# A gMLP and forgetting-attention trunk on one core: the samples' spatial weights turned on VectorE, and the forget gate's running sums as column tiles

## The chip, the core and the metric

The kernel runs on one of the eight cores of a Trainium2 chip. A core has TensorE (PE in the profile: matrix products, and transposes as products with an identity matrix; PEld is its loading of weights), VectorE (DVE), ScalarE (ACT), GpSimd (POOL) and SyncE (SP), which here only issues transfers. Each engine works through its own instructions in order and waits at semaphores for the others. Transfers can also be issued from ScalarE's and GpSimd's queues. SBUF is the on-chip memory with 128 partitions; PSUM is the memory of eight banks into which TensorE writes.

The metric is the device time of one execution in microseconds (us). The times are a median of three runs; the profile is of one execution.

## The reference

One inference step of a two-layer encoder. There are two groups of tokens: a prompt of 512 tokens, and 8 samples of 16 tokens each, 640 tokens in all, which the kernel treats as five tiles of 128 (the fifth holds the samples). Model width 1024, branch width E = 2048. What matters here:

```python
# layer 0, gMLP
proj = h @ w_in                          # (tokens, 3E)
uv = gelu(proj[..., :2*E]); z = proj[..., 2*E:]
u = uv[..., :E]
v = layer_norm(uv[..., E:], ln_g, ln_b)
n = min(T, 128)                          # prompt: blocks of 128; samples: one block of 16
wm = where(chunk_causal_mask(n), w_s[:, :n, :n], 0)
s = einsum('gij,bnjgc->bnigc', wm, vb) + b_s[:, :n].T[...]
y = u * s * silu(z);  out = y @ w_out
# layer 1, forgetting attention
q, k, v, z, logf = ...                   # logf = log_sigmoid(h @ w_f + b_f), one per token and head
cT = cumsum(logf, axis=1).transpose(...) # running sums, 16 heads
s = q @ k * scale + cT[query] - cT[key]; softmax over the causal keys; @ v; * silu(z); @ w_out
```

In layer 0 there are 16 groups g of 128 channels, each with its own 128 x 128 matrix w_s[g]. The samples use the top left 16 x 16 corner of it, the same for all eight samples. In layer 1 the running sums of the forget gate's logarithms over the prompt's 512 tokens form a 16 x 512 table.

## The kernel before

Numbers are 32 bits wide. Most products are made of three: each operand is split into a high part (a copy in the narrower form fp32r) and a low part (the rest), and `mm3` (L270) adds high x high, high x low and low x high (L272, L273, L274). The high half of a split is a ScalarE copy (L289, L292), the low half a VectorE subtraction (L290, L293). Weights come in units of 512 KB into raw buffers (`fetch`, L197), and `prefetch` (L214) splits them into W some items ahead of their use.

**Layer 0.** First v is computed in four panels of 512 channels (L613 on), with its statistics. Then come the groups, in pairs (L768): for the pair's u and then its z, `seven_products` (L707) computes 2 x 128 channels of 640 tokens with seven products instead of eight, in Strassen's manner. Its products use four banks in turn (UZ, L705), and VectorE adds them up (L724 to L735). Between u and z, `spatial_weights` (L680) prepares both groups of the pair. For the prompt, TensorE transposes w_s[g] (L688) and ScalarE copies two parts of it (L690, L691). For the samples, VectorE lays the 16 x 16 corner out as a block-diagonal 128 x 128 matrix: `blk` is one where two tokens are of the same sample, and it is multiplied with the corner repeated along the columns (L684). TensorE transposes that matrix (L689) and ScalarE copies it to SBUF (L692). The block-diagonal matrix has one buffer, `ax`, for all groups. In the first three pairs, panels 1 to 3 of v are normalised after z (`layer_norm_panel`, L651: four ScalarE instructions, two of VectorE's). `gate_spatial` (L737) multiplies with v (L745, L746) and with u and silu(z) on VectorE (L739, L748 to L753).

The 16 x 16 corners of all groups are loaded before the pairs begin into `w16`, by eight small transfers (L668), one for each sample's 16 partitions; the row index i lies on the partitions. The memory below it, from column 10240 of R1, first holds operands of `right_operands` (L575) and later u, z and the spatial weights of two groups.

**Layer 1.** `forget_logits` (L962) computes the forget gate's logits in 32-wide column tiles of the array, each with its own quarter of the 128 partitions of a bank. `log_forget` (L982) takes logarithms, and `forget_sums` (L1003) forms running sums. For the prompt, four products with a triangular matrix of ones add up in one bank to the 16 x 512 table (L1006): the product of token tile t covers all columns from 128 t on. ScalarE copies it to SBUF (L1007) and stores it to a buffer in HBM, c_sc (L1008), from which each head later loads its own row spread over 128 partitions (`load_w0`, L1136). The samples' sums follow (L1009 to L1018).

**Order.** A scheduler orders the instructions of each engine before the kernel runs, by the order of the program and by when it expects operands to be ready. `queued(...)` (L127) keeps an engine's instructions behind a noted one (`behind`). `interleave` (L370) sets pieces of attention between the steps of a projection by times written by hand: `forget_sums` stands at 9.0 in the first value projection (L1353). The work around it is `project_v0`, `project_k0` and the first `project_q` (L1353 to L1359), with a split of summed activations between them (L1356).

Of the kernel before, what the change touches and what calls it, by code (L numbers as in the profile page):

```python
# [24 lines left out]
P = 128  # L25
D = 1024
E = 2048
H = 16
DH = 128
SEQ = 512  # L30
NB = 8
# [26 lines left out]
def hybrid_trunk(tc, x_prompt, x_sample, ck, cv, clf, p_prompt, p_sample, norm_pre, norm_post,  # L58
# [61 lines left out]
    def dma(out, in_, queue=None):  # L120
        if queue is not None:
            queue.dma_start(out=out, in_=in_)
        else:
            behind["sp"] = nc.sync.dma_start(out=out, in_=in_)
# [540 lines left out]
    w16 = r1(o_A, 256).rearrange("p (g j) -> p g j", g=16)  # L665
    assert o_A + 256 <= o_X
    for b in range(NB):
        dma(w16[b * TS:(b + 1) * TS], w_s[0, :, :TS, :TS].rearrange("g i j -> i g j"))  # L668
    for z in range(2):
# [10 lines left out]
    def spatial_weights(g):  # L680
        z = g % 2
        raw, wm, ws, ax = r1(o_wsr + z * P, P), r1(o_wm + z * P, P), r1(o_ws + z * P, P), r1(o_ax, P)
        nc.vector.scalar_tensor_tensor(out=spb[z], in0=spb[z], scalar=lnb[:, g:g + 1], in1=r1(o_bs + z * P, P), op0=ALU.mult, op1=ALU.add)
        nc.vector.tensor_tensor(  # L684
            out=ax.rearrange("p (b j) -> p b j", b=NB), in0=blk.rearrange("p (b j) -> p b j", b=NB),
            in1=w16[:, g:g + 1, :].broadcast_to([P, NB, TS]), op=ALU.mult)
        b = bank(SPA)
        nc.tensor.transpose(out=b[:, :P], in_=raw, identity=ident)  # L688
        nc.tensor.transpose(out=b[:, P:2 * P], in_=ax, identity=ident)  # L689
        nc.scalar.activation(out=wm[0:64, :], in_=b[0:64, 0:P], func=AF.Copy)  # L690
        nc.scalar.activation(out=wm[64:128, 64:128], in_=b[64:128, 64:P], func=AF.Copy)  # L691
        nc.scalar.activation(out=ws, in_=b[:, P:2 * P], func=AF.Copy)  # L692

# [261 lines left out]
    fx3 = fx.rearrange("p (t h) -> p t h", t=NT)  # L955
    cT, ex, cS = r1(o_PT + 288, SEQ, H), r1(o_PT + 800, P), r1(o_V + 1760, 272)
    assert o <= o_K and o_PT + 288 >= o_P + 1280 and o_PTs + 96 >= o_qp + 1280
# [45 lines left out]
    def forget_sums():  # L1003
        pb = bank(ATT)
        for t in range(4):
            nc.tensor.matmul(pb[:H, t * P:], lf3[:, t], tri[:, :SEQ - t * P], start=(t == 0), stop=(t == 3))  # L1006
        nc.scalar.activation(out=cT, in_=pb[:H, :], func=AF.Copy)  # L1007
        dma(c_sc, cT, nc.scalar)  # L1008
        nc.vector.tensor_tensor(  # L1009
# [399 lines left out]
```

## Time and profile before

| | |
|---|---|
| median of three runs | 1272.98 us (1272.37 to 1273.51) |
| the profiled execution's own time | 1273.51 us |
| its span, first to last instruction | 1271.6 us |
| granted TensorE clock | 1.0 |
| blends of the samples' weights (L684) | 16, from 138.1 us of the span on |
| transposes of them (L689) | 16, 140.8 to 336.4 us |
| running sums (L1006) | 8 records, 567.2 to 569.3 us |

A row of a timeline gives start and duration in us, the engine, the line in the kernel, the operation, what it writes and reads by the program's names (R is R1, pb a bank, W the split weights, CST the constants, sf and sff scratch), the shapes, and how many instructions are merged in it. In brackets stands the idle time before it and what ended it. "SPq" and "ACTq" rows are issues of transfers from an engine's queue. A product in 32-bit numbers makes two passes, so the profile shows two records for it. A row of the chain has start, duration, engine, tile and line: it is the path followed back from the last instruction, at each step to what released it or to the instruction before it on its engine. Matmuls are pipelined and their ends are modelled, so the distance between starts says more about TensorE than the durations. The windows view gives each engine's busy time in a stretch, its count of instructions in brackets, then the granted clock, the share of the transfer engines and GB/s.

### The profile page before, as it was taken

The page shows a single profiled execution, that of the slowest core. Times are in us where ns is not written, and L with a number is a line of the kernel's source. Part 1 is how long each engine was busy: PE and PEld are TensorE (multiplying, and loading weights), DVE is VectorE, ACT ScalarE, POOL GpSimd, SP SyncE. Part 2 cuts the span into 40 slices and gives each one's busy share as a digit, 9 for nine tenths or more (in the row PEclk, how much of TensorE's full clock was granted, in tenths as well). Part 3 has the DMA queues.
Part 4 walks back from the last instruction along what each step waited for, and adds up shares of the span by engine and source line. Part 5 has one row for each costly group of instructions (what it writes and reads, how often), then busy time and mean ns, then how long its engine had stood idle before and what let it go on. Part 6 is the DMA issues. An engine that isn't in the chain of part 4 may idle for free.

```text
span 1271.6 us, 21433 instructions
## 1 busy us (share of the span) xinstructions
PE 1264.2 (99%) x8038; PEld 1136.5 (89%) x8038; DVE 957.1 (75%) x1795; ACT 594.6 (47%) x1076; POOL 356.2 (28%) x323
## 2 busy tenths in 40 slices
PE   9999999999999999999999999999999999999998
PEld 7888999999988888889999999999999998788887
DVE  6844999999953364789988998989898988545643
ACT  4433555544545343665445454545454445454331
POOL 1012445454000010145434535454435430000100
PEclk9999999999999999999999999999999999999999
DMA  5532343323324212657798858677888659632211
GB/s 201 174 98 78 108 127 112 103 80 104 114 94 144 94 44 84 150 127 157 173 167 168 195 150 186 157 172 142 151 168 179 177 110 283 230 129 84 67 66 50
DMA packets 275545, 171.54 MB, mean 135 GB/s; under 512 B 188721, under 2 KB 238689, under 8 KB 275442
## 3 DMA queue, kind: packets, MB, share of 16 engines
q1 hardware_dynamic: 261170, 127.80, 36.9%
q0 software_dynamic: 9760, 36.05, 13.7%
q10 hardware_dynamic: 4512, 6.33, 1.7%
q8 instruction: 63, 1.03, 0.3%
q14 instruction: 40, 0.33, 0.1%
HBM read 148.55 MB, written 21.59 MB: 134 GB/s over the span
## 4 chain that ended last, share of the span: by engine, by line
PE 97%; DVE 2%; issue 0%; ACT 0%; ACTq 0%; DVEq 0%
PE pb L272 27%; PE pb L274 27%; PE pb L273 27%; PE pb L1193 3%; PE pb L1270 2%; PE pb L419 2%; PE pb L1186 1%; PE pb L1243 1%; PE pb L317 1%; PE pb L745 1%; PE pb L1058 1%; DVE W L290 1%; PE pb L1071 1%; PE pb L1262 0%; PE pb L1059 0%
## 5 line engine op out<-in xcount | busy, mean ns | idle before, releaser
L272 PE MATMUL pb<-A,W 128*128 128x320 f32 (+1 forms) x752 | 240.7, 320 | 0.0
L273 PE MATMUL pb<-A,W 128*128 128x320 f32 (+1 forms) x752 | 233.7, 311 | 0.0
L274 PE MATMUL pb<-A,W 128*128 128x320 f32 (+1 forms) x752 | 233.2, 310 | 0.0
L290 DVE TENSOR_TENSOR W<-RAW,W 128x1024 fp32r<-128x1024 f32 (+1 forms) x122 | 149.6, 1227 | 71.9 <-ACT W L289 69.7
L273 PE MATMUL pb<-W,A 128*128 128x512 f32 x498 | 194.5, 391 | 0.0
L272 PE MATMUL pb<-W,A 128*128 128x512 f32 x498 | 194.5, 393 | 0.0
L274 PE MATMUL pb<-W,A 128*128 128x512 f32 x498 | 194.3, 391 | 0.0
L289 ACT ACTIVATE W<-RAW 128x1024 fp32r<-128x1024 f32 (+1 forms) x122 | 115.8, 949 | 90.0 <-PE pb L274 43.9
L272 PEld LDWEIGHTS pb<-A,W 128*128 128x128 f32 x752 | 141.6, 188 | 1.0 <-issue 0.2
L273 PEld LDWEIGHTS pb<-A,W 128*128 128x128 f32 x752 | 141.6, 188 | 0.5
L274 PEld LDWEIGHTS pb<-A,W 128*128 128x128 f32 x752 | 141.2, 188 | 0.0
L272 PE MATMUL pb<-tbf,W 128*128 128x320 f32 x360 | 118.9, 330 | 0.4 <-DVE R L1099 0.4
L303 POOL TENSOR_TENSOR SML<-SML 128x1 f32<-128x1 f32 x20 | 14.9, 749 | 350.9 <-DVE SML L301 346.2
L274 PE MATMUL pb<-tbf,W 128*128 128x320 f32 x360 | 111.3, 309 | 0.0
L273 PE MATMUL pb<-tbf,W 128*128 128x320 f32 x360 | 111.2, 309 | 0.0
L274 PEld LDWEIGHTS pb<-W,A 128*128 128x128 f32 x498 | 93.4, 188 | 19.6 <-issue 0.4
L273 PEld LDWEIGHTS pb<-W,A 128*128 128x128 f32 x498 | 93.6, 188 | 18.7
L272 PEld LDWEIGHTS pb<-W,A 128*128 128x128 f32 x498 | 93.5, 188 | 18.5
L211 POOL TENSOR_TENSOR sff<-RAW 128x512 f32<-128x512 f32 x46 | 61.2, 1330 | 169.3 <-DVE W L290 90.7
L713 DVE TENSOR_TENSOR R<-R,pb 128x320 f32<-128x320 f32 x184 | 86.3, 477 | 12.8 <-PE pb L274 11.7
L290 DVE TENSOR_TENSOR A<-R,A 128x640 fp32r<-128x640 f32 (+1 forms) x42 | 35.5, 880 | 57.8 <-ACT A L289 57.8
L272 PEld LDWEIGHTS pb<-tbf,W 128*128 128x128 f32 x360 | 67.7, 188 | 10.3 <-issue 5.8
(270 smaller groups left out, 2842.2 us busy)
## 6 DMA issues: line engine op xcount, KB each, us to landing
RAW<-in_fox_w_in POOLq DMA_DIRECT2D x46, 512.0 KB, 7.5
RAW<-in_gmlp_w_in SPq DMA_DIRECT2D x40, 512.0 KB
R<-in_cache_fox_k SPq DMA_DIRECT2D x128, 128.0 KB
R<-in_cache_fox_v SPq DMA_DIRECT2D x32, 512.0 KB
RAW<-in_gmlp_w_out SPq DMA_DIRECT2D x16, 512.0 KB
RAW<-in_ple_w_gate SPq DMA_DIRECT2D x16, 512.0 KB
RAW<-in_fox_w_out SPq DMA_DIRECT2D x16, 512.0 KB
R<-in_fox_w_in POOLq DMA_DIRECT2D x14, 512.0 KB, 8.5
```

What stands on the lines that cost most here:

```text
L211: nc.gpsimd.tensor_tensor(out=o, in0=a, in1=b, op=op)
L272: nc.tensor.matmul(out, lh, rh, start=start, stop=False)
L273: nc.tensor.matmul(out, lh, rl, start=False, stop=False)
L274: nc.tensor.matmul(out, ll, rh, start=False, stop=stop)
L289: first = nc.scalar.activation(out=hi, in_=src, func=AF.Copy)
L290: nc.vector.tensor_tensor(out=lo, in0=src, in1=f(hi), op=ALU.subtract)
L303: behind["pool"] = nc.gpsimd.tensor_tensor(out=q, in0=t, in1=mhalf, op=ALU.pow)
L317: behind["pe"] = nc.tensor.transpose(out=b[:, j * P:(j + 1) * P], in_=src[:, (4 * c + j) * P:(4 * c + j + 1) * P], identity=ident)
L419: line[e] = make(*args, **kw)
L713: behind["dve"] = nc.vector.tensor_tensor(out=into(i, j), in0=a, in1=b, op=ALU.add)
L1193: nc.tensor.matmul(O[:, d], v[:, j, hh * P:(hh + 1) * P], pt[:, j * P:(j + 1) * P], start=(j == 0), stop=(j == i))
L1270: last = nc.tensor.matmul(O[32 * bl:32 * bl + 32, :256], pt[:, t * P + 32 * bl:t * P + 32 * bl + 32], v_of(p)[:, 4] if t == 2 else vv[:, b ...
```

## The change

The corners are loaded twice side by side, in 16 transfers, so that each block of 32 x 32 elements holds the corner of one group in four copies. VectorE's transpose, which turns each block of 32 x 32 in place, turns all groups at once, and one ScalarE copy takes one of the two copies into `w16`. The column index j then lies on the partitions, and the blend gives the block-diagonal matrix already turned: it is written straight to `ws`, which has two buffers. The transposes on TensorE and ScalarE's copies of them go, and so does `ax`. The two new buffers lie where u of the first pair is written later.

For the forget gate, each of the four blocks of 128 tokens gets its own quarter of the partitions of a bank, with 32 columns of the array (16 heads and 16 that nobody reads). Ten products of 128 columns take the place of four of 512, 384, 256 and 128. ScalarE copies 128 x 128 in place of 16 x 512, and four stores of 16 rows take the place of one.

```diff
+    twice, turned_twice = r1(o_u, 512), r1(o_u + 512, 512)
     for b in range(NB):
-        dma(w16[b * TS:(b + 1) * TS], w_s[0, :, :TS, :TS].rearrange("g i j -> i g j"))
+        for z in range(2):
+            dma(twice.rearrange("p (g z j) -> z p g j", g=16, z=2)[z, b * TS:(b + 1) * TS], w_s[0, :, :TS, :TS].rearrange("g i j -> i g j"))
+    with queued("dve"):
+        nc.vector.transpose(out=turned_twice, in_=twice)
+    nc.scalar.activation(out=w16, in_=turned_twice.rearrange("p (g z i) -> p g z i", g=16, z=2)[:, :, 0], func=AF.Copy)
...
     def spatial_weights(g):
         z = g % 2
-        raw, wm, ws, ax = r1(o_wsr + z * P, P), r1(o_wm + z * P, P), r1(o_ws + z * P, P), r1(o_ax, P)
+        raw, wm, ws = r1(o_wsr + z * P, P), r1(o_wm + z * P, P), r1(o_ws + z * P, P)
...
         nc.vector.tensor_tensor(
-            out=ax.rearrange("p (b j) -> p b j", b=NB), in0=blk.rearrange("p (b j) -> p b j", b=NB),
+            out=ws.rearrange("p (b j) -> p b j", b=NB), in0=blk.rearrange("p (b j) -> p b j", b=NB),
             in1=w16[:, g:g + 1, :].broadcast_to([P, NB, TS]), op=ALU.mult)
         b = bank(SPA)
         nc.tensor.transpose(out=b[:, :P], in_=raw, identity=ident)
-        nc.tensor.transpose(out=b[:, P:2 * P], in_=ax, identity=ident)
...
-        nc.scalar.activation(out=ws, in_=b[:, P:2 * P], func=AF.Copy)
...
-    cT, ex, cS = r1(o_PT + 288, SEQ, H), r1(o_PT + 800, P), r1(o_V + 1760, 272)
+    cT, ex, cS = r1(o_PT + 288, P), r1(o_PT + 800, P), r1(o_V + 1760, 272)
...
     def forget_sums():
         pb = bank(ATT)
         for t in range(4):
-            nc.tensor.matmul(pb[:H, t * P:], lf3[:, t], tri[:, :SEQ - t * P], start=(t == 0), stop=(t == 3))
-        nc.scalar.activation(out=cT, in_=pb[:H, :], func=AF.Copy)
-        dma(c_sc, cT, nc.scalar)
+            for g in range(t, 4):
+                nc.tensor.matmul(pb[32 * g:32 * g + 32, :P], lft[:, t * H:t * H + 32], tri[:, (g - t) * P:(g - t + 1) * P],
+                                 start=(t == 0), stop=(t == g))
+        nc.scalar.activation(out=cT, in_=pb[:, :P], func=AF.Copy)
+        for g in range(4):
+            dma(c_sc[:, g * P:(g + 1) * P], cT[32 * g:32 * g + H], nc.scalar)
```

## The prediction

> **What bounds the kernel now.** I read the page first: the engines' totals and the chain that ended last.
>
> ```profile
> span 1271.6 us, 21433 instructions
> PE 1264.2 (99%) x8038; PEld 1136.5 (89%) x8038; DVE 957.1 (75%) x1795; ACT 594.6 (47%) x1076; POOL 356.2 (28%) x323
> PE 97%; DVE 2%; issue 0%; ACT 0%; ACTq 0%; DVEq 0%
> ```
>
> TensorE (PE) carries 97% of the chain, so a slot taken from PE is worth its length wherever PE itself is the limit. The other 2% of the chain is VectorE (DVE), so the second question is whether the edited places lie there. I asked for the busy times of three stretches: two pairs of groups whose second half also normalises a panel (groups 2 and 3, 4 and 5; groups 0 and 1 are the third such pair), and one of the five pairs without.
>
> ```profile
> core 0: us, PE busy (x) PEld busy (x) DVE busy (x) ACT busy (x) POOL busy (x), PEclk, DMA share, GB/s
> 162.70:190.40 27.70, 27.57 (x192) 27.29 (x192) 27.03 (x40) 15.53 (x28) 12.94 (x9) 1.00 0.40 121
> 190.40:218.10 27.70, 27.57 (x192) 27.29 (x192) 27.05 (x40) 15.52 (x28) 12.93 (x9) 1.00 0.37 117
> 251.20:278.50 27.30, 27.30 (x195) 27.27 (x193) 25.16 (x40) 12.69 (x24) 12.79 (x9) 1.00 0.29 89
> ```
>
> The pair without a panel is PE's: busy 27.30 of 27.30, VectorE 25.16. The two with a panel are nearly VectorE's too: 27.03 and 27.05 busy of 27.70, and they last 0.40 longer. The clock is full (1.00) in all. The same view around the forget gate's running sums:
>
> ```profile
> 565.00:573.00 8.00, 7.59 (x42) 5.47 (x41) 7.90 (x10) 5.76 (x9) 5.45 (x3) 1.00 0.61 104
> ```
>
> Here VectorE is busy 7.90 of 8.00 and PE is the one with gaps.
>
> **The samples' transposes.** Gone are 16 transposes (L689) and 16 ScalarE copies (L692); the blend (L684) stays and writes the buffer itself. In the chain a transpose is a short step between product steps:
>
> ```profile
> 131.49 0.22 PE pb L688 x2
> 251.31 0.11 PE pb L689
> 251.42 0.15 PE pb L274
> ```
>
> Two take 0.22, one takes 0.11: 16 x 0.11 = 1.76 us of PE's order. In the five pairs without a panel PE has no idle time, so 10 x 0.11 = 1.1 comes back in full. In the three with a panel PE loses time once per pair, like this:
>
> ```profile
> 162.23 0.31 PE L274 MATMUL pb<-A,W 128*128 128x320 f32 x1
> 162.70 0.41 PE L272 MATMUL pb<-tb,W 128*128 128x320 f32 x1 [0.16 <-DVE R L726]
> 145.61 0.34 issue
> 145.95 1.07 ACT W L289
> 147.04 1.59 DVE L290 TENSOR_TENSOR W<-RAW,W 128x1024 fp32r<-128x1024 f32 x1 [0.26 <-ACT W L289]
> ```
>
> The step from 162.23 to 162.70 is 0.47 where the chain's product steps take 0.15: PE waits until VectorE has emptied a bank. VectorE's long run before that wait does not begin by itself: the chain reaches it at 145.95 through a ScalarE split that comes 0.34 after the last PE step. I read that split as waiting for PE to release a weight buffer, and so what PE saves before it moves VectorE's run as well; the spare time there is small, 0.26 before the split's VectorE half at 147.04, so 0.22 a pair just fits. I take 6 x 0.11 = 0.66 for these pairs; at worst 0. ScalarE's 16 copies were beside other work: it is busy 12.69 of 27.30, so their going brings nothing.
>
> **The blend without its wait.** The two groups shared one buffer, so the second blend waited for the first transpose. It now needs a buffer last read a pair earlier, and may stand right behind the first:
>
> ```profile
> L684 DVE TENSOR_TENSOR R<-CST,R x16: 278/984/1393, 138.1 to 333.5; 128x128 f32<-128x128 f32 x16
> 166.15 1.39 DVE L684 TENSOR_TENSOR R<-CST,R 128x128 f32<-128x128 f32 x1
> 167.73 1.21 DVE L290 TENSOR_TENSOR W<-sf,W 128x1024 fp32r<-128x1024 f32 x1
> 169.86 0.98 DVE L684 TENSOR_TENSOR R<-CST,R 128x128 f32<-128x128 f32 x1
> 163.70 2.23 POOL L211 TENSOR_TENSOR sf<-sf,RAW 128x512 f32<-128x512 f32 x1
> 166.01 1.38 POOL L211 TENSOR_TENSOR sf<-RAW,sf 128x512 f32<-128x512 f32 x1
> 169.94 0.31 PE L272 MATMUL pb<-tb,W 128*128 128x320 f32 x1
> ```
>
> The same blend takes 0.28 to 1.39; the 1.39 lies beside GpSimd's (POOL's) 166.01 to 167.39. Moved ahead of the split at 167.73, it delays that split, done at 168.94, and the product that needs it at 169.94; queued behind it are also the bank emptyings. Slack 1.0, blend 0.28 to 0.98: covered, cost 0; a blend of 1.39 would leave PE waiting 0.4. If it meets GpSimd differently, the change in VectorE's time per pair lies between -1.1 and +1.1 (0.28 against 1.39); I take 0, nearest to the mean, since GpSimd's work is the same. The Trainium skill (SBUF — State Buffer, Who interferes with whom) says that a VectorE instruction with two SBUF inputs and a GpSimd one that reads SBUF share a port pair, and whichever starts first holds it to its end. The 1.39 beside 1.38 agrees; by that rule the moved blend could also wait out a whole 2.23, which would use up the slack and cost PE some 1.2 in a pair.
>
> **The turn.** Added: eight more small loads on SyncE's queue (SP), one VectorE transpose of 128 x 512, one ScalarE copy of 128 x 256.
>
> ```profile
> 62.80 1.82 SPq L124 DMA_DIRECT2D R<-in_gmlp_w_s  x4
> 65.46 0.38 SPq L124 DMA_DIRECT2D RAW<-in_gmlp_w_in  x1
> 83.74 1.06 ACT L289 ACTIVATE W<-RAW 128x1024 fp32r<-128x1024 f32 x1 [4.00 <-issue]
> 126.42 0.26 DVE L644 BATCH_NORM_AGGREGATE SML<-SML 128x2 f32<-128x24 f32 x1
> 132.90 0.48 DVE L713 TENSOR_TENSOR R<-R,pb 128x320 f32<-128x320 f32 x1
> 574.24 0.83 DVE L1085 STREAM_TRANSPOSE R<-R 128x640 f32<-128x640 f32 x1
> 142.42 0.49 DVE L726 TENSOR_TENSOR R<-R,pb 128x320 f32<-128x320 f32 x1 [0.58 <-PE pb L274]
> 143.42 1.23 DVE L290 TENSOR_TENSOR W<-sf,W 128x1024 fp32r<-128x1024 f32 x1 [0.52 <-ACT W L289]
> ```
>
> A load takes 1.82 / 4 = 0.46 to issue, eight more take 3.6. Behind them queue a weight fetch (65.46) and the first groups' weights, which are not used before 131. The raw buffers are a ring of three; by their order that fetch is split at 83.74, 18 us after its issue: cost 0, and if that cover were gone at most 3.6. The transpose is 512/640 x 0.83 = 0.66, behind the last panel's statistics at 126.42; VectorE still has 0.58 and 0.52 idle ahead of the first pair's long run, so it is taken up: cost 0, at most 0.66. The copy is under 0.4 of a ScalarE that is half idle. The first total written over these buffers waits for the copy, but it comes at 132.90, over 6 us after those statistics.
>
> **The running sums.** Before, 1280 columns in two passes each, twenty blocks of 128, one after another; after, the same twenty blocks in four quarters, the deepest of which has four products, eight passes.
>
> ```profile
> 567.30 2.26 PE pb L1006 x8
> 548.21 0.65 PE L968 MATMUL pb<-R,WF 128*32 128x128 f32 x16
> 567.43 2.58 DVE L290 TENSOR_TENSOR A<-R,A 128x1280 fp32r<-128x1280 f32 x1
> 569.93 2.30 DVE L293 SCALAR_TENSOR_TENSOR W<-RAW,W 128x1024 fp32r<-128x1024 f32 x1
> 572.16 0.41 DVE L1099 TENSOR_TENSOR R<-R,pb 128x256 f32<-128x256 f32 x1
> 570.06 0.41 PE L273 MATMUL pb<-A,W 128*128 128x320 f32 x1
> 572.62 0.41 PE L272 MATMUL pb<-tbf,W 128*128 128x320 f32 x1 [0.38 <-DVE R L1099]
> 570.65 0.38 ACTq L1018 DMA_DIRECT2D cs_sc<-R  x1
> 577.01 0.31 ACT L1114 ACTIVATE R<-R 128x128 f32<-128x128 f32 x1 [4.06 <-DMA R<-cs_sc]
> ```
>
> The nearest row is L968, which already runs 128-column passes in quarters: 16 in 0.65, where one after another at 0.11 they would take 1.76. So eight deep is 8 x 0.11 = 0.88, and PE's step shrinks from 2.26 by about 1.3 (0 if the quarters run one after another). The Trainium skill (TensorEngine Tiling (Array Packing), Theoretical Speedup) allows up to four times for 32 columns. By it the step would be 0.57 and shrink by 1.7; L968's 2.7 times is the nearer figure.
>
> But does PE profit? Behind the sums it needs the low half written at 567.43 to 570.01: its second product of that kind starts at 570.06, 0.05 after. Then it needs the bank that L1099 frees at 572.57, and starts at 572.62, 0.05 after. VectorE has next to no idle time up to there (7.90 of 8.00, above), and none of these three instructions reads the sums. So PE would come 1.3 earlier and wait 1.3 longer: I take 0, nearest to those two rows; at best 1.3. ScalarE's copy gets shorter, and three more stores cost 3 x 0.38 = 1.1 of its queue; behind them stand a split, the loads of the sums and an instruction that today follows 4.06 of idle time. Cost 0.
>
> **Sum.** Median 1272.98, the profiled execution 1273.51 (its span 1271.6 and 1.9 around it). Against the profiled one: 1273.51 - 1.1 - 0.66 - 0 + 0 = 1271.75; it stands 0.53 above the median, so 1271.2 for the median. A difference under 0.2% (2.5 us) is about what a measurement of this kernel cannot tell from none.
>
> **The rivals.**
>
> *Both savings count.* The chain itself puts the sums (2.26) on the path and hops from PE to VectorE at 569.93, which speaks for it; VectorE's unbroken run, which that split only queues in, speaks against. If VectorE's order comes out so that the bank is emptied ahead of the two long splits, 1.3 more comes back: 1269.9. The Trainium skill (Perfetto Trace Analysis, Identifying the Most-Contended Engine) advises working on the most occupied engine first; PE at 99% would then give all it is relieved of.
>
> *VectorE pays in the pairs with a panel; slower.* Its idle time there is 0.67 of 27.70. If the moved blend is blocked as the first is (1.39 for 0.98, +0.4) and the split it displaces falls on GpSimd (one of 128x1024 took 2.30 at 569.93, for the 1.21 at 167.73: +1.1), a pair gains 1.5 of VectorE work; three make 4.5, less the 1.1 of the other pairs: 1272.98 + 3.4 = 1276.4. It decides once VectorE's added time in a pair passes its idle time. For it speak blends of 0.98 and more already; against it, that the pair's GpSimd work is unchanged and another instruction goes free.
>
> *Nothing comes back from these pairs.* Their length is VectorE's, the six transposes there turn into wait, and the turn's 0.66 is uncovered: 1272.98 - 1.1 + 0.66 = 1272.5.
>
> **How the numbers follow.** Forecast 0.45, both savings 0.23, slower 0.15, nothing back 0.17. The time is the likeliest case's, 1271.2. The low end is both savings and a further 1.0 for the three waits of about 0.32 like that at 162.70: 1268.9. The high end is 1.95 of VectorE's loss (three times 0.65, less than half the rival's), less 1.1, and 0.5 for the spread of the runs: 1274.3. That leaves out the slower case and little else. Faster by over 0.2%: the case of both savings and a small part (0.05) of the forecast, 0.28. Slower: 0.15. The rest, 0.57.
>
> **What would show it.** Right: no L689, pairs without a panel 0.22 shorter, those with one 0.1 to 0.22 shorter; the sums' step near 0.9, and a wait of PE for VectorE behind it that is 1.3 longer than the present ones. Wrong: if the next product after the sums starts over 1 us earlier relative to VectorE's splits; if pairs with a panel grow; or if instructions around the edits stand in another order on VectorE, which my sum assumes they do not, beyond the blend.

## The result: 0.65% slower

The kernel after takes 1281.38 us (median of 6 runs, 1281.18 to 1282.2), the kernel before, run beside it, 1273.55 (6 runs, 1272.37 to 1274.27). The ratio is 1.0065 (95% interval 1.0053 to 1.0076). The forecast was 1271.2 with a range up to 1274.3. The profiled execution of after took 1281.24 with a span of 1279.3, that of before 1273.51 with 1271.6: 7.7 us more. One execution among all that follow, of e13 below, ran at a granted clock of 0.851 and is left out of its ratio.

The page of the profile after, totals and chain:

```profile
PE 1262.8 (99%) x8034; PEld 1136.3 (89%) x8034; DVE 958.9 (75%) x1796; ACT 591.1 (46%) x1061; POOL 352.2 (28%) x323
PE 91%; DVE 4%; DMA 2%; issue 1%; ACT 1%; SPq 0%; DVEq 0%; ACTq 0%
```

TensorE has 1.4 us less work (1262.8 for 1264.2) in a longer span, and transfers, absent from the chain before, hold 2% of it. To see where, I followed TensorE's position: the start of each of its steps after, less that of the same step before. It is -0.73 at the first of the 16 spatial steps (131 us), -0.43 at the end of layer 0 (344), -0.41 just ahead of the running sums (566.8), -1.05 at 593, +8.35 at 628, and +7.88 at the end. The first figure is not the change's: three experiments below (e2, e7, e10) whose program up to there is that of before have -1.02, -0.94 and -0.43. That leaves +0.30 from layer 0, where the forecast had -1.76; -0.64 from the sums, where it had 0; and **+9.4 between 593 and 628, in a stage that the change does not edit and the prediction does not treat.** Behind it, -0.47 comes back. Of the windows after (columns as in the prediction), a stretch with a panel and the stage that lost, with the clock in and behind its wait:

```profile
162.70:190.40 27.70, 26.82 (x187) 26.31 (x186) 27.01 (x40) 14.90 (x26) 11.74 (x9) 1.00 0.39 118
575.00:607.00 32.00, 25.17 (x170) 24.06 (x169) 22.25 (x49) 12.64 (x24) 13.29 (x12) 0.89 0.73 139
596.40:600.00 3.60, 0.00 (x1) 0.00 (x0) 0.65 (x2) 0.00 (x0) 0.00 (x0) 1.00 0.27 68
600.00:606.80 6.80, 3.57 (x14) 3.57 (x14) 6.80 (x15) 2.18 (x6) 4.46 (x3) 0.50 0.49 77
```

Before, the stretch from 575 to 607 is:

```profile
575.00:607.00 32.00, 32.00 (x240) 29.65 (x239) 29.80 (x69) 16.93 (x33) 15.80 (x16) 1.00 0.84 175
```

In the stretch with a panel TensorE has 26.82 of 27.70 where it had 27.57. In the stage its 32.00 become 25.17 and VectorE's 29.80 become 22.25: both wait for something else. The granted clock is 0.89 over it: TensorE stands still from 596.4 to 603.2 (6.83, below), and the clock is 0.50 from 600.0 to 606.8. The Trainium skill (TensorE: Matmul & The Clock Gate, Part 1: The HAM clock gate) says that the clock halves after an idle window of some 3.4 us and comes back after as long of work; the trace agrees (it halves 3.6 us into the wait and is full again 3.6 us after its end).

**Layer 0.** The five pairs without a panel are 0.22 shorter each, as forecast. In the three with a panel VectorE's position loses 0.78 each, and TensorE's changes by -0.10, +0.75 and +0.78; with the five that makes the +0.30. These are the pairs of groups 2 to 7, not 0 to 5 as the prediction has it: the panels' ScalarE rows before (L654) start at 152, 180 and 208 us, in the first halves of those pairs. Rows of the timeline before, ScalarE, VectorE and GpSimd:

```profile
167.66 0.61 ACT L289 ACTIVATE W<-R 128x512 fp32r<-128x512 f32 x1
168.83 0.27 ACT L690 ACTIVATE R<-pb 64x128 f32<-64x128 f32 x1 [0.23 <-PE pb L689]
168.86 0.68 DVE L290 TENSOR_TENSOR W<-R,W 128x512 fp32r<-128x512 f32 x1
169.02 1.68 POOL L211 TENSOR_TENSOR sf<-R 128x512 f32<-128x512 f32 x1 [1.62 <-DVE W L290]
```

And after, with the wait of TensorE that follows:

```profile
166.80 0.25 ACT L694 ACTIVATE R<-pb 64x128 f32<-64x128 f32 x1
...
167.82 0.63 ACT L289 ACTIVATE W<-R 128x512 fp32r<-128x512 f32 x1
168.36 1.30 POOL L211 TENSOR_TENSOR sf<-R 128x512 f32<-128x512 f32 x1 [1.83 <-DVE W L290]
168.48 1.72 DVE L290 TENSOR_TENSOR W<-R,W 128x512 fp32r<-128x512 f32 x1 [0.20 <-ACT W L289]
188.08 0.42 PE L272 MATMUL pb<-A,W 128*128 128x320 f32 x1 [0.64 <-DVE R L727]
```

Before, ScalarE split first (167.66) and copied the transposed weights later, since those stood behind the second transpose. Without that transpose all four copies (166.80 to 167.82) stand ahead of the split. Its VectorE half then starts 0.12 behind GpSimd's addition (168.48 against 168.36) and takes 1.72 for 0.68. Before, it started 0.16 ahead of that addition, and it was the addition that took longer, 1.68 for 1.30. The second blend, on the other hand, takes 0.28 in place of 0.98.

**The sums.** The timeline of TensorE after:

```profile
566.82 1.08 PE L1010 MATMUL pb<-CST,R 128*32 128x128 f32 x20
569.66 0.42 PE L273 MATMUL pb<-A,W 128*128 128x320 f32 x1 [1.19 <-DVE A L290]
573.13 0.31 PE L272 MATMUL pb<-tbf,W 128*128 128x320 f32 x1
```

The step shrinks from 2.26 to 1.01 (566.82 to 567.83), and TensorE waits 1.19 for the low half: both as forecast. But the second wait, for the bank that L1105 (L1099 before) frees, has gone: another series of products now runs first, and that bank's product starts at 573.13, long after it is free.

**The stage that lost.** The chain of waits after, in order of time (start, duration, what):

```profile
574.71 9.84 DMA out<-R
...
584.57 0.32 SPq L124
...
588.18 11.05 DMA R<-in_cache_fox_k
...
599.35 1.42 DVE R L1225 x4
```

Four loads of 128 KB bring the keys that VectorE transposes at 599.35 (L1225; L1219 before). The timeline of after around them:

```profile
586.53 3.50 SPq L124 DMA_DIRECT2D R<-in_cache_fox_k  x4
586.95 0.77 POOL L122 DMA_DIRECT2D R<-in_fox_w_in  x1
599.35 1.42 DVE L1225 STREAM_TRANSPOSE R<-R 128x256 f32<-128x256 f32 x4 [6.34 <-DMA R<-in_cache_fox_k]
602.19 1.45 POOL L211 TENSOR_TENSOR sff<-RAW,R 128x512 f32<-128x512 f32 x1 [10.39 <-DVE W L290]
603.23 0.69 PE L272 MATMUL pb<-W 128*128 128x384 f32 x1 [6.83 <-DVE SML L1178]
603.91 2.31 DVE L290 TENSOR_TENSOR W<-RAW,W 128x1024 fp32r<-128x1024 f32 x1
606.14 1.57 DVE L1129 SCALAR_TENSOR_TENSOR R<-R 128x320 f32<-128x320 f32 x1
```

And of before:

```profile
585.32 16.31 SPq L124 DMA_DIRECT2D R<-in_cache_fox_k  x8
587.63 0.77 POOL L122 DMA_DIRECT2D RAW<-in_fox_w_in  x1
591.96 1.41 DVE L1219 STREAM_TRANSPOSE R<-R 128x256 f32<-128x256 f32 x4
596.50 1.21 DVE L290 TENSOR_TENSOR W<-RAW,W 128x1024 fp32r<-128x1024 f32 x1
599.11 1.48 POOL L211 TENSOR_TENSOR sff<-RAW,R 128x512 f32<-128x512 f32 x1 [8.29 <-DVE R L1180]
```

Before, the fourth key load goes out at 586.95, 0.68 ahead of the first of two weight fetches of 512 KB on GpSimd's queue (587.63), and all four land 2.4 to 3.1 us after their issue; VectorE does not wait. After, the fetch at 586.95 comes between the first load and the second (586.97). The first lands in 2.43, the others in 7.55, 7.66 and 11.05, and VectorE idles 6.34. It resumes late enough to meet GpSimd's next additions, and beside them a split takes 2.31 for 1.21 and the product behind it 1.57 for 0.48: 2.2 more. TensorE stands still for 6.83. The chain passes from VectorE to TensorE only at 608.98, so the halved clock lies beside it.

Two things brought the loads behind the fetch. The fetch moved up in GpSimd's order, ahead of its last addition. And the loads moved back on SyncE's queue: in the chain a store (584.57) is held until one issued at 574.71 has landed, 9.84 later, because the program hands its semaphores out in turn and the next transfer with the same one waits for it. Before, that landing took 8.23. It ends shortly after the second of two weight fetches issued near 573.5, which itself took 10.54 after and 8.84 before. Also, a load of 512 KB of values moved two stores up on that queue.

### The profile page after: what moved, and what is told of

Its sections match the earlier page's. It is cut to its first block, busy times and chain, and to the rows that moved or that the text cites. A ratio compares the mean times of both kernels' runs of the same rounds, so it can differ in the third digit from the quotient of the medians.

```text
span 1279.3 us, 21439 instructions
## 1 busy us (share of the span) xinstructions
PE 1262.8 (99%) x8034; PEld 1136.3 (89%) x8034; DVE 958.9 (75%) x1796; ACT 591.1 (46%) x1061; POOL 352.2 (28%) x323
## 4 chain that ended last, share of the span: by engine, by line
PE 91%; DVE 4%; DMA 2%; issue 1%; ACT 1%; SPq 0%; DVEq 0%; ACTq 0%
PE pb L272 26%; PE pb L274 25%; PE pb L273 25%; PE pb L1199 3%; PE pb L1276 2%; PE pb L419 2%; PE pb L1192 1%; PE pb L1249 1%; PE pb L317 1%; DVE W L290 1%; DMA R<-in_cache_fox_k 1%; PE pb L748 1%; DMA out<-R 1%; PE pb L1064 1%; PE pb L1077 1%
```

## The experiments

Sixteen kernels. None leaves out or changes any of the computation. "Position" is TensorE's, against before, from one profiled execution each; "start" is its value at 131 us. Kernels that were timed together (e1 to e4, e5 to e8, e9 to e12, e13 and e14, e15 and e16) share their runs of before.

### Each part alone

e1 is the change with `forget_sums` as before (theory A: the loss belongs to the sums' part), e2 the change with the spatial weights as before.

> The change's first part alone: corners loaded twice and turned, blends straight to their place, no transposes; the running sums as before. Theory A (the loss sits in layer 1 and comes from the sums part, which moved one transfer on SyncE's queue and one on GpSimd's): this part is worth what layer 0 shows in the changed kernel, -0.73 ahead of the first raw transposes, -0.22 in five pairs, about +1.4 over the three pairs whose first half ends a panel, together -0.4: 1273.1 where the kernel before is 1273.5, and each of the second four key loads lands within 3.2 us. Theory B (the eight more loads shift the hand-out of the transfers' semaphores and so layer 1): about 1281, and a key load that takes 11 us.

> The change's second part alone: running sums by tiles in the quarters of a bank, four stores; layer 0 as before. Theory A: the whole loss, +9.4 at the second key turn, less 0.6 that the shorter sums give and 0.45 near the end: 1281.8 where the kernel before is 1273.5, VectorE waits over 6 us for key loads. Theory B: no loss here, about 1272.5.

e1: 1279.45, ratio 1.0042 (1.0028 to 1.0055). e2: 1279.16, 1.0040 (1.0020 to 1.0059). Theory A falls: each part alone loses most of it. Theory B (the eight added loads shift the semaphores) falls as the only cause, since e2 has none of them. e1's layer 0 is +0.29, as with both parts; then it loses 5.2 between 593 and 628, though it leaves the order on GpSimd's queue and the place of the value load as they were. Its timeline:

```profile
588.20 0.77 POOL L122 DMA_DIRECT2D RAW<-in_fox_w_in  x1
594.04 1.43 DVE L1222 STREAM_TRANSPOSE R<-R 128x256 f32<-128x256 f32 x4 [1.43 <-issue]
599.67 2.31 DVE L290 TENSOR_TENSOR W<-RAW,W 128x1024 fp32r<-128x1024 f32 x1
```

The fourth key load went out at 588.14, 0.07 ahead of this fetch, and took 5.82. VectorE waits only 1.43 for it; most of the rest goes on three instructions that now run beside GpSimd's additions (1.37, 2.31 and 1.55 for 0.28, 1.21 and 0.48 before). In e2 the fetch (585.72) stands ahead of the second load and VectorE idles 5.09, but the sums themselves gain 0.64 (-1.04 to -1.68), as with both parts.

### Putting one order back

From after, with parts of each edit shown (e5's and e6's other lines are left out): e3 issues the value load behind the stores that it had overtaken (theory A1: it is the value load); e4 holds the fetch behind GpSimd's addition; e5 sends the last four key stores from GpSimd's queue, so that the keys need not queue behind them; e6 issues the value load behind the keys.

```diff
# e4
+            with queued(*["add"] * (state["raw"] == S2 + 11)):
                 dma(raw_of(state["raw"])...
...
# e5
...
+            store_k(h, both(o_vk, h), nc.gpsimd if h else None)
# e6
+    def keys_then_values():
+        with queued("sp"):
+            load_k(0, 1, 0)
+            with queued("sp"):
+                load_v(0, 0, (1,))
...
```

> The changed kernel, but the load of the second half of the cached values stands behind four of the second head's key stores on SyncE's queue, as in the kernel before, and not behind two; GpSimd's queue stays as changed, with one weight fetch ahead of the last addition. Theory A1 (the place of the value load alone makes the key loads late): 1272.0, that is 1273.5 - 0.4 - 0.64 - 0.45, and VectorE waits under 0.5 us for the keys. Theory A2 (the weight fetch that moved ahead of an addition decides, the value load only adds 1.2 us): fetch at about 585.7, key loads at 585 to 586.6, so one or two of the four still land behind it: 1274 to 1278. Theory C (the four stores or the earlier TensorE alone, whatever the order): 1281.

> The changed kernel, but the weight fetch that moved ahead of GpSimd's last addition is held behind that addition again; SyncE's queue stays as changed, with the value load behind two stores. Theory A1 (the place of the value load alone): still about 1281. Theory A2 (the fetch decides): fetch at about 588.3 instead of 586.9, the key loads of 586.5 to 588.2 go first and land within about 3.5 us: 1272 to 1274. Theory C (stores or the earlier TensorE, whatever the order): 1281.

> The changed kernel, but the last four of the second head's eight key stores are issued from GpSimd's queue, so that the four key loads behind them leave SyncE's queue up to 2 us earlier (about 584.6 to 586.3); all else stands in the changed kernel's order. So far every variant lost 5 to 9 us at the same place, also the one in which all transfers stand in the order of the kernel before. Theory R (a race: the last of the four key loads is issued within 0.1 us of a 512 KB weight fetch from GpSimd's queue, or after it, and then lands 6 to 11 us later; the kernel before wins the race by 0.68 us, and any shift of a microsecond loses it): the loads win again, VectorE waits under 1 us for the keys, 1272 to 1274 where the kernel before is 1273.5. Theory O (an order of products, splits or stores in the changed kernel makes layer 1 slower whenever the keys land): still 1279 to 1281.

> The changed kernel, but the load of the second half of the cached values stands behind the eight key stores and the four key loads on SyncE's queue; all else in the changed kernel's order. Theory R: without its 512 KB ahead of them the stores land some 2 us earlier, the key loads are issued at about 584.5 and win: 1272 to 1275 (above 1273 if the value load now delays the weight fetch). Theory O: still 1279 to 1281.

e3: 1280.81, 1.0049 (1.0032 to 1.0066); e4: 1279.02, 1.0039 (1.0025 to 1.0054); e5: 1279.0, 1.0034 (1.0021 to 1.0047); e6: 1277.72, 1.0021 (1.0006 to 1.0036). Theories A1 and A2 both miss, and no single order gives the time back. Theory C (late whatever the order) fits e3 by its time, and theory O fits e5; theory R expected 1272 to 1274 in e5 and 1272 to 1275 in e6. Only the traces, and e7 and e13 below, tell them apart. In e3 two loads still go out behind the fetch; in e4 the fourth goes out 0.07 behind it and takes 8.25; in e5 0.17 ahead and takes 7.79. In e6 all four are ahead and land in at most 3.21; VectorE no longer waits for them but for another small load, the mask from `cs_sc`:

```profile
583.21 0.18 DVE L1246 TENSOR_TENSOR R<-R,CST 128x16 f32<-128x16 f32 x1 [2.36 <-DMA R<-cs_sc]
```

That load was issued 0.03 behind a weight fetch of the round before (572.35) and took 10.81; before, it was issued 0.37 ahead of it and took 5.04. So the theory became: there is a race of small loads against 512 KB fetches (theory R), and it is run twice; before wins both, by chance.

### The kernel before made to lose

e7 is before with the last two key stores cut in two: two transfers more on SyncE's queue, the same bytes, nothing of the change.

```diff
...
-            store_k(h, both(o_vk, h))
+            store_k(h, both(o_vk, h), 2 if h else 1)
```

> The kernel before, with the last two of the second head's key stores each cut into two halves: two transfers more on SyncE's queue, 0.9 us ahead of the four key loads, the same bytes, nothing else moved. Theory R: the 0.68 us by which the last key load is ahead of the weight fetch are gone, it lands 3 to 8 us later, and the kernel before becomes 1277 to 1281. Theory O: 1273.5, no difference.

1278.68 against 1273.51, ratio 1.0031 (1.0019 to 1.0042). Its timeline:

```profile
585.01 13.98 SPq L124 DMA_DIRECT2D R<-in_cache_fox_k  x8
586.57 0.77 POOL L122 DMA_DIRECT2D RAW<-in_fox_w_in  x1
594.49 1.42 DVE L1224 STREAM_TRANSPOSE R<-R 128x256 f32<-128x256 f32 x4 [3.51 <-DMA R<-in_cache_fox_k]
```

The fourth load is issued at 586.69, 0.11 behind the fetch, and takes 7.68. Theory R holds and theory O (no difference) falls: the loss needs no part of the change. Over all kernels the fourth load behaves like this:

| kernel | issued ahead of the first fetch, us | landing, us | VectorE idle before the keys, us |
|---|---|---|---|
| e10 | 3.81 | 3.24 | 0 |
| e15 | 1.32 | 3.30 | 0 |
| before | 0.68 | 3.11 | 0 |
| e11 | 0.66 | 3.34 | 0 |
| e16 | 0.49 | 3.08 | 0 |
| e6 | 0.41 | 3.21 | 0 |
| e13 | 0.28 | 3.63 | 0 |
| e14 | 0.21 | 4.58 | 0.10 |
| e5 | 0.17 | 7.79 | 1.52 |
| e1 | 0.07 | 5.82 | 1.43 |
| e8 | -0.02 | 6.57 | 2.27 |
| e12 | -0.05 | 6.74 | 2.46 |
| e4 | -0.07 | 8.25 | 4.04 |
| e7 | -0.11 | 7.68 | 3.51 |
| e3 | -1.02 | 10.27 | 5.34 |
| e9 | -1.08 | 10.06 | 5.20 |
| after | -1.23 | 11.05 | 6.34 |
| e2 | -1.35 | 9.69 | 5.09 |

From 0.28 to 0.17 ahead the landing doubles. In the ten kernels at 0.17 or less TensorE's position loses 3.6 (e8) to 9.4 us (after) from 593 to 628. The trace of after shows what the loads meet: its view of the queues (packets, MB, share of the 16 transfer engines) for 588 to 589, first line, and 590 to 591, when three key loads are under way:

```profile
q1 hardware_dynamic: 1426, 0.18, 115.1%
...
q0 software_dynamic: 37, 0.15, 95.4%
q1 hardware_dynamic: 34, 0.00, 2.7%
```

The keys move in packets of 128 bytes on the hardware queue, the fetch in packets of 4 KB on GpSimd's. Once the fetch's packets come, the keys fall from 1426 packets in a microsecond to 34, beside 37 of the fetch's. The Trainium skill (DMA: Bandwidth & Descriptors, Queues, rings and completion order) says that a transfer engine takes turns between queues by packets. By it a load of small packets beside a fetch gets a small share of each engine until the fetch is through; the packets and the landings agree, but no run here changes the packets' size.

### Layer 0

From the first part alone: e8 holds the second blend behind z's first addition in the pairs with a panel (theory V: the blend delays VectorE's split); e12 holds ScalarE's four copies behind z's first product copy there (theory C: the copies delay ScalarE's split).

```diff
# e12
...
             if n == 0:
-                nc.scalar.activation(out=m1, in_=o, func=AF.Copy)
+                behind["act"] = nc.scalar.activation(out=m1, in_=o, func=AF.Copy)
+                with queued(*["act"] * bool(late)):
+                    while late:
+                        late.pop(0)()
```

> The change's first part alone, with the second group's blend held behind the first addition of z in the three pairs (2, 4, 6) whose first half ends a panel, as in the kernel before; one look. Theory V (the blend that moved ahead puts a 128 x 512 split beside GpSimd's additions, 1.73 instead of 0.68, and costs VectorE 0.78 in each of the three pairs): from the first raw transposes to the last spatial product TensorE is 1.7 us ahead of the kernel before instead of 0.3 behind, and that split takes 0.7. Rival (the loss comes from the transposes that are gone: TensorE arrives earlier and waits): still within 0.5 of the kernel before. In layer 1 it may lose the race for the keys like the others.

> The change's first part alone, with ScalarE's four copies of the transposed weights held behind its copy of z's first product in the pairs 2, 4 and 6; the blends free; one look. The blend held behind the addition recovered 0.4 of 2.3 only; its trace showed ScalarE's half of the 128 x 512 split a microsecond later than in the kernel before, behind the four copies, and VectorE's half beside GpSimd's addition (1.52 instead of 0.68). Theory C (the copies in front of the split cost VectorE 0.8 a pair): split's half back at 0.7, TensorE 1.5 to 2 us ahead of the kernel before from the first raw transposes to the last spatial product. Rival (the blend in front of it delays the split by 0.28 anyway and that is enough to meet the addition): still within 0.8 of the kernel before. In layer 1 it may lose the races like the others.

One execution each. e8 changes its position by -0.08 over layer 0 and the split stays at 1.51: theory V falls. (Its time is 1278.88; some 2.4 of it go from 668 on, in six steps of some 0.4, and their cause stays open.) e12 changes it by -1.48 (-0.95 to -2.43), 0.22 in each pair without a panel and 0.10 to 0.14 in each with one, and the split is itself again:

```profile
167.42 0.26 ACT L698 ACTIVATE R<-pb 64x128 f32<-64x128 f32 x1
167.99 0.68 DVE L290 TENSOR_TENSOR W<-R,W 128x512 fp32r<-128x512 f32 x1
168.15 1.68 POOL L211 TENSOR_TENSOR sf<-R 128x512 f32<-128x512 f32 x1 [1.83 <-DVE W L290]
```

The split starts 0.16 ahead of GpSimd's addition again. Theory C holds: with the copies behind, the first part gives back nearly what the forecast said (-1.76). Its time is still 1275.91, since in layer 1 the fourth key loses by 0.05 us and 4.2 goes.

### All orders held

e9 is e6 with the mask load put ahead of the two row loads on ScalarE's queue. e10 makes the orders of e9 in before. e11 is e9 with e4's fetch and e12's copies held as well. e13 is e11 with the two fetches in the order of before, RAW first. e14 holds only the fetches' order and the copies.

```diff
# e9
...
+            behind["mask"] = nc.scalar.dma_start(out=r1(o_Ws, 272), in_=cs_sc[:8]...)
+        with queued("mask"):
             load_w0(0, nc.scalar)
...
# e13
...
+            u = {S2 + 11: S2 + 12, S2 + 12: S2 + 11}.get(state["raw"], state["raw"])
+            ap, k = units[u]
...
```

> The changed kernel, with the small transfers ahead of the large ones on both queues: the load of the samples' mask (136 KB written, VectorE needs it near 582) stands ahead of the two 256 KB loads of the first heads' sums on ScalarE's queue, and the second half of the cached values behind the key loads on SyncE's. Theory R2 (two races against GpSimd's 512 KB fetches: the keys' and the mask's; in the run with the values last the keys won, and the mask, issued 0.03 us behind a fetch, still landed at 583.2 instead of 578 and held VectorE 2.4 us): mask landed by 578, keys by 590.5, no idle of VectorE over 0.7 us from 574 to 600, and 1272 to 1274 where the kernel before is 1273.5. Rival O (something else in the changed order makes the stage slower): 1276 or more although both land in time.

> The same order of transfers in the kernel before: mask first, values last; nothing of the change. Theory R2: the kernel before already wins both races, so this order gains it nothing: 1273 to 1274. Rival O2 (the value load behind the keys has a price of its own, as it now stands beside the weight fetches): 1275 or more, and the run above must be read against this one.

> The run with the mask first and the values last, and besides the weight fetch held behind GpSimd's last addition and, in the pairs 2, 4 and 6, ScalarE's four copies of the transposed weights held behind its copy of z's first product. Theory R2 with the copies: layer 0 gains 1.8 from the first raw transposes to the last spatial product instead of losing 0.3, so 1270 to 1272. Rival: the copies are not what costs VectorE there, and this run is at most 0.3 below the one with the mask first.

> The run in which all was held (mask first, values last, fetch behind the addition, ScalarE's copies behind z's first product), with one more thing: the two neighbouring weight fetches on GpSimd's queue change places, as they stand in the kernel before; no other instruction moves on any queue. That run won both races and still lost 1.9 us of its 3.0 at 597.5. Theory G (GpSimd's next three additions start when the fetch issued first lands, 592.7 there and 599.1 in the kernel before; they then run beside VectorE's split and addition, which took 2.32 and 1.58 instead of 1.21 and 0.48): with the fetches swapped the additions start after 596.5, that split takes 1.2 again, TensorE's wait of 2.0 at 597.5 shrinks under 0.4, and the time is 1271.5 to 1272.5 where the run before it had 1273.8. Rival W (the later weights are then missed by TensorE): a wait for a split of them near 603 takes the place, 1273.5 to 1275.

> The changed kernel with only two of these edits: ScalarE's copies held in the pairs 2, 4 and 6, and GpSimd's queue in the order of the kernel before (addition, then the two fetches as they stand there). The value load stays ahead of six of the second head's key stores and the mask behind the two row loads. Theory R2: layer 0 gives 1.5, the mask still loses (lands near 582) and the keys are issued within 0.5 us of the fetch, so that it can go either way: 1273 to 1279, and TensorE loses over 2 us more between 590 and 610 than in the run with the mask first and the values last. Rival: the places of the mask and of the values do not matter once GpSimd's queue is as before: 1271.5 to 1272.5.

**e9**: 1279.72, 1.0046 (1.0029 to 1.0063), where theory R2 (two races) expected 1272 to 1274. The mask wins, but a fetch (585.44) now goes out ahead of the third and fourth key, and VectorE idles 5.20.

**e10**: 1281.43, 1.0052 (1.0037 to 1.0067), where 1273 to 1274 was expected, for a reason that I had not seen. A row load behind the mask has the semaphore of a store that had not landed; its issue held ScalarE until 582.07:

```profile
582.07 0.32 ACTq L122 DMA_DIRECT2D sff<-c_sc  x1
...
582.94 0.51 ACT L1116 ACTIVATE R<-R 128x128 f32<-128x128 f32 x2 [10.43 <-DMA out<-R]
```

**e11**: 1273.76, 0.9993 (0.9981 to 1.0005), where 1270 to 1272 was expected. Layer 0 is -1.50, both races are won, the position at 593 is -2.96 (start -0.85); then 1.9 goes. Its timeline:

```profile
592.73 1.48 POOL L212 TENSOR_TENSOR sff<-RAW,R 128x512 f32<-128x512 f32 x1 [3.97 <-DVE W L291]
594.49 2.32 DVE L291 TENSOR_TENSOR W<-RAW,W 128x1024 fp32r<-128x1024 f32 x1
596.73 1.58 DVE L1144 SCALAR_TENSOR_TENSOR R<-R 128x320 f32<-128x320 f32 x1
599.59 0.44 PE L1207 MATMUL pb<-CST,R 128*128 128x128 f32 x2 [1.72 <-DVE R L1201]
```

The R fetch, now first, lands at 592.44, so GpSimd's additions start at 592.73, over 6 us earlier than before (599.11), beside VectorE's split and product: 2.32 for 1.21 and 1.58 for 0.48. The next theory (G) was that R second would bring those additions back behind them.

**e13**: median 1271.2 against 1274.14; nine of its twelve times lie between 1269.6 and 1272.0, three at 1278.8, 1283.3 and 1378.0. The first two of these make the interval wide: 0.9991 (0.9968 to 1.0014). Its timeline:

```profile
586.17 0.77 POOL L203 DMA_DIRECT2D RAW<-in_fox_w_in  x1
590.49 1.41 DVE L1244 STREAM_TRANSPOSE R<-R 128x256 f32<-128x256 f32 x4
595.03 1.21 DVE L295 TENSOR_TENSOR W<-RAW,W 128x1024 fp32r<-128x1024 f32 x1
597.68 1.44 POOL L216 TENSOR_TENSOR sff<-RAW,R 128x512 f32<-128x512 f32 x1 [8.33 <-DVE R L1205]
```

No wait for the keys, no addition beside the split. The position is +0.08 at the start, -1.47 after layer 0, -2.08 at 593 and still at 1034, -2.28 at the end. Theory G holds, and theory C of e3 and e4 falls: this kernel has the four stores and the earlier TensorE, and the stage loses nothing. The profile is of one of the nine.

**e14**: 1275.7, 1.0006 (0.9988 to 1.0023). Its keys cost next to nothing (0.10), but the mask does (VectorE idle 1.19), and a store (2.37); the position goes from -2.24 to +0.92. So holding the fetches and the copies alone does not do, as theory R2 expected.

### What eight early loads do to transfers 500 us later

The first part issues eight more loads from 60 us on. Theory Q: their number alone, through what it does to later transfers, lengthens the fetches near 573. e15 is before with eight loads of the corners that nobody reads; e16 is the first part with the copies held and eight loads instead of sixteen, ScalarE making the second copy.

```diff
# e16
-        for z in range(2):
-            dma(twice.rearrange(...)[z, b * TS:(b + 1) * TS], ...)
+        dma(twice.rearrange(...)[0, b * TS:(b + 1) * TS], ...)
+    tw = twice.rearrange("p (g z j) -> z p g j", g=16, z=2)
+    nc.scalar.activation(out=tw[1], in_=tw[0], func=AF.Copy)
```

> The kernel before, with the corners loaded a second time into memory that nobody reads before u: eight more small loads on SyncE's queue in layer 0, 500 us ahead of the key loads; no instruction of another engine moves, and all transfers of layer 1 stand in the same order. In the runs with the change's first part alone the second of the two weight fetches near 573 took 9.65 to 10.2 us, in those without it 8.0 to 8.8, and that microsecond is what lost the race for the keys. Theory Q (the count of transfers that went before is enough, by how the later ones fall upon the 16 transfer engines): that fetch takes 9.6 or more, the last key load 5 us or more, 1277 to 1281. Rival N (something else of the first part): 8.0 to 8.9 and 1273 to 1274.

> The run of the change's first part with ScalarE's copies held, but with eight loads of the corners as in the kernel before; the second copy of them is made on chip by one ScalarE copy of 128 x 256. Theory Q: the second fetch near 573 is back at 8.0 to 8.9, the keys are issued over 0.5 us ahead of the next fetch and win, and what layer 0 gives (1.5) is kept to the end: 1271.5 to 1272.5. Rival N: the fetch still takes 9.6 or more, a key load 5 us or more: 1275 to 1278.

e15: 1277.7 (1273.0 to 1279.0), 1.0019 (1.0004 to 1.0035). Eight unused loads slow before. Its keys win, but the second fetch near 573 takes 10.74 (8.84 before) and the mask load 11.00:

```profile
582.94 0.18 DVE L1242 TENSOR_TENSOR R<-R,CST 128x16 f32<-128x16 f32 x1 [2.92 <-DMA R<-cs_sc]
```

e16: 1272.42, 0.9988 (0.9973 to 1.0003). Both races are won, layer 0 gives -1.47, and the position at the end is -2.23 (start -0.87). With e11 and e13 it is one of three versions at or below before in these measurements; none of their intervals excludes no change. But its second fetch takes 9.21, between before's 8.84 and e12's 10.18, and more than I expected. So eight more loads are enough to slow before; by what way they reach so far stays open. That they lengthen the second fetch is not shown: in single executions it takes 9.15 to 11.4 in kernels with the added loads and 7.99 to 9.51 (e2) in those without; how a transfer's pieces fall on the 16 engines was not tried. e15's runs reach down to 1273.0, so the outcome differs between executions too. So do those of before: of its 108 executions beside all these kernels 11 took over 1277 us, up to 1282.53, and no trace of one was kept.

## Why the prediction was wrong, point by point

**The step that failed.** The sum holds terms for the edited places only. It assumes that every other stage keeps its time, and costs the transfers by the queues that issue them ("eight more take 3.6 ... cost 0", "three more stores ... Cost 0"). The stage from 575 to 607, of which the prediction reads a single row (577.01, for the mask's cover), had loads that beat a fetch by 0.68 us. The change moved both sides of that race, and +9.4 is there; everything else, the start's -0.73 among it, comes to -1.5. The trace of before had it to be read: SyncE's key loads from 585.32 and the fetch at 587.63, with VectorE's transpose at 591.96 behind them. e7 shows that two small transfers lose it without the change, e13 that the whole change with the orders held does not lose it. A wait for late keys is also not the whole price: what VectorE then does beside GpSimd's additions makes up 2.2 of the 9.4 in after and most of e1's 5.2. Which transfer moved first is not one thing: e3, e4 and e6 each put one back and none suffices.

**Transposes in the pairs without a panel:** right, 0.22 each.

**In the pairs with a panel:** wrong. The forecast was 0.22 gained and at worst 0; VectorE lost 0.78. What failed is "their going brings nothing" of ScalarE's copies: those that remained moved ahead of a split that VectorE needs. The text named another order of instructions as what would make it wrong, but on VectorE; it was ScalarE's. The sum also had the pairs wrong (groups 2 to 7, not 0 to 5). The rival for slower had the price (a split beside GpSimd, +1.1; measured 1.72 for 0.68, +1.04), but not the place: it blamed the blend, which became cheaper (0.28 for 0.98), and e8 clears it. The Trainium skill (SBUF — State Buffer, Who interferes with whom), cited there for the blend, agrees: the split takes 1.72 where GpSimd's 1.30 starts 0.12 ahead of it, and 0.68 where it starts 0.16 ahead and GpSimd's takes 1.68. With the copies held such a pair gives 0.10 to 0.14 of the 0.22 (e12).

**The turn:** no cost shows at its place, as forecast. One of 0.66 could not be told, since the positions at 131 us scatter by over 1 us, with the turn (-1.31 to +0.08) and without (-1.06 to 0). Its eight loads are e15's matter.

**The sums:** the step of 0.88 was 1.01, and the first wait came as forecast. "PE would come 1.3 earlier and wait 1.3 longer" failed in its second half: with another order of products on TensorE the bank was free in time, and 0.64 came back where 0 was taken.

**The total, had orders stayed:** e13's position gains 1.55 in layer 0, where the sum has 1.76, 0.62 at the sums, where it has 0, and 0.20 behind them. So layer 0's size was about right once the order was held; the sums' was not, and the cover of all other stages failed. That e13's median, 1271.2, is the forecast's figure is luck: its terms are others.

## What to carry to other kernels

Before costing a small edit, list the small loads that go out shortly before a large fetch from another queue, with their margin in us, in the stages behind the edit too: here kernels with a margin of 0.17 us or less lost 3.6 to 9.4 us, and those with 0.21 or more next to nothing to the keys. An edit that removes instructions also moves those that remain, so compare the order on every engine and queue, ScalarE's among them, and hold it by hand before judging the edit itself. A kernel that wins such races by chance is no firm base: its own time moves by 0.3% with two transfers more (e7).

## What the runs showed of the hardware

The fourth load of 128 KB of keys lands in 3.1 to 3.6 us in the kernels that issue it 0.28 us or more ahead of a 512 KB fetch from GpSimd's queue, in 4.58 at 0.21, and in 5.8 to 11.05 at 0.17 or less. The margin is not all: e14's third load, 0.82 ahead, takes 4.75, and e10's first three 4.4 to 4.7 beside loads on ScalarE's queue and with no fetch under way. A VectorE split of 128 x 512 takes 0.68 where it starts 0.16 us ahead of a GpSimd addition, which then takes 1.68, and 1.72 where it starts 0.12 behind one of 1.30. An issue whose semaphore is still out holds everything behind it on its engine: in after a store and the keys, until a store issued 9.84 us earlier had landed; in e10 ScalarE, 10.43 us idle. And loads added at 60 us went with longer transfers at 573 in the one execution that was profiled: 10.74 and 11.00 for 8.84 and 5.04 (e15).
